# Rebuilding the state-space parameters in wider instructions, and moving the last modulation steps of a four-layer block program behind the next norm

## The chip, the cores and the metric

The program runs on one core of a Trainium2 chip. The metric is the device time of one execution in microseconds (us). Five engines have an instruction queue each and run it in order: PE (matrix products; its weight loads are shown as PEld), DVE (vector), ACT (scalar functions and copies), POOL and SP. In this program SP issues the weight loads (DMA queue q1) and POOL issues small and modulation loads (q0). Engines wait for each other by semaphores; an instruction that waits holds back everything behind it on its engine.

## The reference, cut to what matters

One sequence of 256 tokens with 1024 features goes through two *first* layers and then through a *second* block of two layers.

```python
# first block, two layers
h = rms_norm(x, pre_norm[l]);  proj = h @ w_in[l]          # attention and long convolution on parts of proj
x = x + rms_norm(m @ w_out[l], post_norm[l])               # the end of a first layer
# second block
def adaln(c, w, b):                                        # "modulation": 3072 columns, four times
    m = silu(c) @ w + b;  return split(m, 3)               # shift, scale, gate
x = x + g * even_mixer(rmsnorm(x) * (1 + sc) + sh, ...)    # layer 0: attention mixer
x = x + g * swiglu(rmsnorm(x) * (1 + sc) + sh, ...)        # layer 0: dense FFN, width 2816
x = x + g * s5_mixer(rmsnorm(x) * (1 + sc) + sh, ...)      # layer 1: state-space mixer
x = x + g * moe_swiglu(rmsnorm(x) * (1 + sc) + sh, ...)    # layer 1: 8 experts
```

The state-space mixer scans `x_t = a x_{t-1} + (f b) u_t` with complex `a`, `f`, `b`, reads out with complex `c` and adds `d_skip * u`. The kernel works on four tokens at a time and needs, from `a, f, b, c, d`, four tables per quarter q of the groups: B (input weights times powers of a), C (output weights times powers of a), K (the direct effect of the tokens of one group of four on each other, a product of C and B plus the diagonal d) and T (rotations). They depend on parameters only, not on x.

## The kernel before, in words

Stages follow each other in time: first layer 0 (to about 288 us), first layer 1 (to 562), even mixer (to about 725), dense FFN (to about 946), state-space mixer (to about 1056), experts (to the end). The 256 tokens are two tiles `tt` of 128. A projection (`proj_tok`, `proj_T`) loads weights by `wchunk` (raw tile by DMA from SP, high part `whi` on ACT at L208, rest `wlo` on DVE at L211) and runs each product as three matmuls, L221 to L223, from `hTh`, `hTl` (high part and rest of the transposed input) and `whi`, `wlo`.

**Between two stages** stands a norm. `x_done(tt)` computes row statistics of tile tt, makes the diagonal `dg` (L421) and lets PE transpose and scale x by it (`transposed`, L440: 8 instructions per tile, 16 records, since each such product is run in two passes). The result goes through `hh` into `hTh` (ACT) and `hTl` (DVE), and the next stage's matmuls can start. `hold` and `held` make the splits of the next stage's first weight chunks issue only after a given ACT instruction: before, the last row statistics of tile 1, for two chunks (`HOLDP` is 2 for a plain norm, `HOLDC` 0 for the one before the state-space mixer).

**Side tasks** are generators. `tick()` in the projections' loops advances each by its rate, `finish()` runs them to their end. One is `modulations()`: for each of the four modulations it runs `adaln`. There, eight times, three weight tiles `rawm` of 128x1024 are loaded by POOL (L945; only three such buffers exist), 24 matmuls with 32-column weights multiply them into four column groups of PE (L959, 48 records), ACT copies the sums to `ads` (L963), and POOL sends them by four small DMAs to `adp` (L965). After the eighth, PE transposes `adp` (L970), DVE forms the columns (L971 to L975) and PE transposes them once more (L977). Another side task is `s5_params`, which runs in the dense FFN and builds the four tables, one quarter after another; its K product is L1500: per quarter 16 matmuls with 128x128 weights and 32 moving columns, 32 records.

**The order** on each engine is set when the kernel is built: a scheduler with a timeline of its own places the instructions, in the order of emission where nothing else decides; `issue_after` and `gate` tie instructions to others, and `first()` gives priority.

## Time and profile before

| | us |
|---|---|
| median of three runs | 1911.8 (1909.59 to 1914.67) |
| the profiled execution | 1902.7 |
| its span, first to last instruction | 1900.2 |
| PE busy in the span | 1818.4 (96%) |
| DVE busy | 1554.9 (82%) |
| ACT busy | 1213.4 (64%) |
| POOL busy | 164.6 (9%) |
| mean granted PE clock, share of full | 0.965 |

The profiled execution is 9.1 us shorter than the median of the runs. A row of the timeline has start and length of a piece of work, engine, line, operation, the tiles `out<-in`, shapes, how many records are put together (x), and, in brackets, how long the engine had been idle before it and what ended that. Matmul records overlap: the pace of PE is read from the starts. A matmul with 512 moving columns starts every 0.23 us at full clock, one with 256 every 0.117 us.

### The profile page before, as it was taken

Reading aid. Unit: us, or ns where it says so; the run is one execution under the profiler, and the core shown is the slowest. Engines: PE = TensorE matmul, PEld = TensorE weight load, DVE = VectorE, ACT = ScalarE, POOL = GpSimd, SP = SyncE. Lnnn points to the kernel's source line nnn. Section 1 sums busy time; section 2 is a strip of 40 time slices with the busy share of each in tenths; the row PEclk is TensorE's granted clock in tenths of the full one; section 3 lists DMA queues with packets and bytes.
Section 4 is the critical chain, followed back from the end, with each engine's and each line's share of the span. In section 5 each row is a group of like instructions: output and inputs, shape, how many; then the busy total and the mean of one; then the engine's idle time right before and its main releaser. Section 6 shows DMA issues by size and latency. Waiting matters only on the chain.

```text
span 1900.2 us, 31269 instructions
## 1 busy us (share of the span) xinstructions
PE 1818.4 (96%) x11358; PEld 1551.7 (82%) x11358; DVE 1554.9 (82%) x2646; ACT 1213.4 (64%) x1708; POOL 164.6 (9%) x297
## 2 busy tenths in 40 slices
PE   7999998999989998999989899999999999999996
PEld 6887776988878778999889788888888888888784
DVE  6887667687558669998678789999999999998996
ACT  5664355564448535555554677887778787877774
POOL 0003232231330000000000100000001000100000
PEclk9999998999999969999988999999999999999998
DMA  7656785876775504787675779999999999999990
GB/s 247 205 153 209 245 286 197 277 259 196 255 242 159 165 22 156 227 270 241 208 284 196 279 266 376 340 355 344 378 342 349 353 377 354 346 369 361 339 352 24
DMA packets 258539, 503.58 MB, mean 265 GB/s; under 512 B 23346, under 2 KB 101108, under 8 KB 256328
## 3 DMA queue, kind: packets, MB, share of 16 engines
q1 hardware_dynamic: 239384, 448.05, 68.7%
q0 software_dynamic: 18992, 53.45, 7.9%
q8 instruction: 91, 1.49, 0.3%
q14 instruction: 72, 0.59, 0.1%
HBM read 485.47 MB, written 15.75 MB: 264 GB/s over the span
## 4 chain that ended last, share of the span: by engine, by line
PE 78%; issue 10%; DVE 6%; DMA 4%; ACT 2%; POOL 0%; POOLq 0%; ACTq 0%; DVEq 0%
PE A L222 12%; PE A L221 12%; PE A L223 12%; PE B L221 6%; PE B L222 6%; PE B L223 6%; PE A L323 4%; PE A L325 4%; PE A L324 4%; PE B L959 2%; DMA rawm<-in_e_mod_mix_w_dram 2%; DVE wlo L211 1%; PE B L1754 1%; PE B L1101 1%; PE B L440 1%
## 5 line engine op out<-in xcount | busy, mean ns | idle before, releaser
L211 DVE TENSOR_TENSOR wlo<-raw,whi 128x1024 fp32r<-128x1024 f32 x777 | 930.8, 1222 | 183.7 <-ACT whi L208 172.0
L208 ACT ACTIVATE whi<-raw 128x1024 fp32r<-128x1024 f32 x777 | 814.3, 1058 | 344.6 <-PE A L223 137.7
L221 PE MATMUL A<-whi,hTh 128*128 128x512 f32 (+1 forms) x752 | 286.7, 389 | 7.5 <-ACT hTh L208 4.9
L222 PE MATMUL A<-wlo,hTh 128*128 128x512 f32 (+1 forms) x752 | 290.0, 386 | 1.3 <-DVE wlo L211 1.0
L223 PE MATMUL A<-whi,hTl 128*128 128x512 f32 (+1 forms) x752 | 287.5, 384 | 0.9 <-DVE hTl L211 0.9
L323 PE MATMUL A<-hTh,whi 128*128 128x256 f32 x864 | 246.2, 285 | 3.5 <-ACT hTh L208 2.6
L325 PE MATMUL A<-hTh,wlo 128*128 128x256 f32 x864 | 245.2, 284 | 0.0
L324 PE MATMUL A<-hTl,whi 128*128 128x256 f32 x864 | 244.1, 283 | 1.0 <-DVE hTl L211 1.0
L221 PEld LDWEIGHTS A<-whi,hTh 128*128 128x128 f32 x752 | 142.9, 190 | 38.8 <-ACT hTh L208 6.1
L323 PEld LDWEIGHTS A<-hTh,whi 128*128 128x128 f32 x864 | 165.4, 192 | 6.9 <-ACT hTh L208 2.8
L222 PEld LDWEIGHTS A<-wlo,hTh 128*128 128x128 f32 x752 | 143.1, 190 | 33.9 <-DVE wlo L211 4.8
L223 PEld LDWEIGHTS A<-whi,hTl 128*128 128x128 f32 x752 | 142.6, 190 | 31.2 <-DVE hTl L211 2.1
L324 PEld LDWEIGHTS A<-hTl,whi 128*128 128x128 f32 x864 | 165.3, 191 | 3.2 <-DVE hTl L211 1.2
L325 PEld LDWEIGHTS A<-hTh,wlo 128*128 128x128 f32 x864 | 165.1, 191 | 1.7 <-issue 1.2
L222 PE MATMUL A<-wlo,xg 128*128 128x512 f32 (+1 forms) x384 | 143.1, 373 | 0.3 <-DVE wlo L211 0.3
L223 PE MATMUL A<-whi,xg 128*128 128x512 f32 (+1 forms) x384 | 142.7, 372 | 0.0
L221 PE MATMUL A<-whi,xg 128*128 128x512 f32 (+1 forms) x384 | 141.2, 375 | 0.0
L222 PE MATMUL B<-wlo,mhh 128*128 128x512 f32 x352 | 138.6, 394 | 0.0
L223 PE MATMUL B<-whi,mhl 128*128 128x512 f32 x352 | 137.5, 391 | 0.0
L221 PE MATMUL B<-whi,mhh 128*128 128x512 f32 x352 | 120.6, 393 | 0.2 <-ACT mhh L208 0.2
L222 PEld LDWEIGHTS A<-wlo,xg 128*128 128x128 f32 x384 | 72.3, 188 | 13.4 <-DVE wlo L211 0.8
L223 PEld LDWEIGHTS A<-whi,xg 128*128 128x128 f32 x384 | 72.3, 188 | 12.5
(588 smaller groups left out, 2868.9 us busy)
## 6 DMA issues: line engine op xcount, KB each, us to landing
raw<-in_o_exp_up_dram SPq DMA_DIRECT2D x176, 512.0 KB, 5.7
raw<-in_o_exp_down_dram SPq DMA_DIRECT2D x176, 512.0 KB, 6.0
raw<-in_o_exp_gate_dram SPq DMA_DIRECT2D x174, 512.0 KB, 5.8
raw<-in_w_in_dram SPq DMA_DIRECT2D x96, 512.0 KB, 4.8
rawm<-in_e_mod_mix_w_dram POOLq DMA_DIRECT2D x24, 512.0 KB, 6.0
rawm<-in_e_mod_ffn_w_dram POOLq DMA_DIRECT2D x24, 512.0 KB, 5.7
rawm<-in_o_mod_mix_w_dram POOLq DMA_DIRECT2D x24, 512.0 KB, 5.6
rawm<-in_o_mod_ffn_w_dram POOLq DMA_DIRECT2D x24, 512.0 KB, 6.3
```

The lines of the kernel that those rows point to most:

```text
L208: nc.scalar.activation(hi, src, AF.Copy)
L211: (nc.gpsimd if lo_eng == "pool" else nc.vector).tensor_tensor(lo, src, hi.bitcast(F32), ALU.subtract)
L221: nc.tensor.matmul(out, ah, bh, start=first, stop=False)
L222: nc.tensor.matmul(out, ah, bl, start=False, stop=False)
L223: nc.tensor.matmul(out, al, bh, start=False, stop=last)
L323: nc.tensor.matmul(o, wh[:, ms], xh[:, k, :], start=k == 0 and m == 0, stop=False, **kw)
L324: nc.tensor.matmul(o, wh[:, ms], xl[:, k, :], start=False, stop=False, **kw)
L325: nc.tensor.matmul(o, wl[:, ms], xh[:, k, :], start=False, stop=k == 7, **kw)
L440: nc.tensor.matmul(o, x[:, ks], dg, start=True, stop=True)
L959: nc.tensor.matmul(acc[32 * j:32 * j + 32, cs], silu[:, k:k + 1].broadcast_to([P, 32]), raws[i][:, k * P:(k + 1) * P], start=r == 0 and i ...
L1101: nc.tensor.matmul(pt[:, i, :], z[ps, ts], w[ps, ts], start=True, stop=True)
L1754: nc.tensor.transpose(ptr[:, i * P:(i + 1) * P], sg[:, i * P:(i + 1) * P], self.ident)
```

## The change

1. `s5_params`: the complex products that were made power by power are made for three or four powers in one instruction (128x384, 128x512), T for two quarters at once (`TQ` = 2); masks are applied by ACT while it copies; the tables' transposes are copied out of PSUM by ACT, not DVE. K is now 16 matmuls per quarter with 32-column weights and 128 moving columns, in four column groups of PE; it is written by 16 small DMAs per quarter from POOL, not by one from SP.
2. The projection `w_out` at the end of both first layers runs `quiet`: no `tick()` in it. After layer 0 one modulation step follows; at layer 1 the `finish(self.adalns)` ahead of the projection is gone, and all steps left are emitted behind the norm that follows, without priority (`urgent` false).
3. `hold` is now the last ACT instruction of tile 0's `transposed`; the first chunk's split is spared from it, the next two are held.

```diff
+    def finish_step(self, gen):
+        for t in list(self.tasks):
+            if t[0] is gen:
+                self.step(t)
@@ wchunk
-            with self.tc.issue_after(self.hold) if self.held > 0 else nullcontext():
+            with self.tc.issue_after(self.hold) if self.held > 0 and self.spared <= 0 else nullcontext():
                 self.split(hi, lo, raw, lo_eng="pool" if self.pool_lo >= 0 else "dve")
-            self.held -= 1
+            if self.spared > 0:
+                self.spared -= 1
+            else:
+                self.held -= 1
@@ proj_tok
-                if k0 + kk < kt and not (trail and c + wd == ncols):
+                if k0 + kk < kt and not (trail and c + wd == ncols or quiet):
                     self.tick()
-            self.tick()
+            if not quiet:
+                self.tick()
@@ x_done
             if tt:
-                self.hold, self.held = self.latest(mybir.EngineType.Activation), HOLDP if kind == "plain" else HOLDC
+                self.hold, self.held, self.spared = self.behind0, HOLDP if kind == "plain" else HOLDC, 1
             self.transposed(tt, x, dg)
+            self.behind0 = self.latest(mybir.EngineType.Activation)
@@ first_layer
-        if l == 1:
-            self.finish(self.adalns)
-        self.proj_tok(mT, a["w_out"][l], 0, D, 8, emit_out, trail=True)
+        self.proj_tok(mT, a["w_out"][l], 0, D, 8, emit_out, trail=True, quiet=True)
+        if l == 0:
+            self.urgent = False
+            self.finish_step(self.adalns)
+            self.urgent = True
@@ first_block
+            self.urgent = False
+            self.finish()
             self.gate = []
-            self.finish()
@@ adaln
-            with self.first():
+            with self.first(self.urgent):
@@ s5_params, B and the products
-            for s in range(3):
-                p = pw[:, 3 - s]
-                self.cmul(sp, [P, 8, 16], bc(p[:, 0, :], 16), bc(p[:, 1, :], 16), W[:, 0, :, 3, :], W[:, 1, :, 3, :],
-                          W[:, 0, :, s, :], W[:, 1, :, s, :], "s5cm")
+            self.cmul(sp, shape, *p, *w, W[:, 0, :, 0:3, :], W[:, 1, :, 0:3, :], "s5cw")
-                V.tensor_tensor(B[:, i:i + 2].rearrange("p a b c -> p (a b) c"), pt.rearrange("p (n c) -> p n c", n=4),
-                                bm[:, None, 0, :].broadcast_to([P, 4, P]), ALU.mult)
+                nc.scalar.copy(B[:, i:i + 2].rearrange("p a b c -> p (a b) c"), pt.rearrange("p (n c) -> p n c", n=4))
@@ s5_params, K
-            for i in range(8):
+            for h in range(2):
                 for ri in range(2):
-                    nc.tensor.matmul(pt[:, i * 32:(i + 1) * 32], W2[:, ri, i].rearrange("p s g k -> p (s g k)"),
-                                     cm[:, ri, i].rearrange("p g k -> p (g k)"), start=ri == 0, stop=ri == 1)
+                    for i in range(4):
+                        nc.tensor.matmul(pt[32 * i:32 * i + 32, h * P:(h + 1) * P], W2[:, ri, 4 * h + i, 3].rearrange("p g k -> p (g k)"),
+                                         C[:, 4 * h + i, ri, 0:4].rearrange("p t g k -> p (t g k)"), start=ri == 0, stop=ri == 1,
+                                         skip_group_check=True)
-            self.dq.dma_start(self.sK[q], K.rearrange("p a b -> p (a b)"))
+                for i in range(4):
+                    self.mq.dma_start(self.sK[q][s * 32:(s + 1) * 32].rearrange("k (h i m) -> k i h m", h=2, i=4)[:, i],
+                                      K[i * 32:(i + 1) * 32, :, 3 - s:7 - s].rearrange("k h t m -> k h (t m)"))
```

In the changed kernel some lines have other numbers: L959 is L973, L440 is L450, L221 to L223 are L226 to L228, L970 and L977 are L984 and L991, L945 is L959, L963 and L965 are L977 and L979.

**PE between first layer 1 and the even mixer, before.** From the last `w_out` matmul on: `adp` and `adb` are the modulation's two transposes, `dg,x` the norm's transposes of tile 0, `whi_6487` and so on the chunks of the mixer's first weights.

```order
L223 MATMUL A_6273<-whi_6306,hTl_6083 128x512
L970 MATMUL B_6180<-ident_78,adp_5451 128x96
L977 MATMUL B_6187<-ident_78,adb_5448 8x128
L440 MATMUL B_6385<-dg_6383,x_75 128x128 x4
L440 MATMUL B_6397<-dg_6383,x_75 128x128 x4
L221 MATMUL A_6483<-whi_6487,hTh_6365 128x512
L222 MATMUL A_6483<-wlo_6488,hTh_6365 128x512
L223 MATMUL A_6483<-whi_6487,hTl_6366 128x512
```

**The same place on PE in the changed kernel**, from the second tile's transposes on; ahead of them stand tile 0's transposes and six matmuls of `whi_6487`. `rawm` are the modulation weights.

```order
L450 MATMUL B_6341<-dg_6327,x_75 128x128 x4
L973 MATMUL B_6353<-rawm_6041,silu_1264 32x128 x8
L973 MATMUL B_6353<-rawm_6040,silu_1264 32x128 x8
L973 MATMUL B_6353<-rawm_6039,silu_1264 32x128 x8
...
L973 MATMUL B_6390<-rawm_6386,silu_1264 32x128 x8
L973 MATMUL B_6390<-rawm_6385,silu_1264 32x128 x8
L973 MATMUL B_6390<-rawm_6384,silu_1264 32x128 x8
L973 MATMUL B_6427<-rawm_6423,silu_1264 32x128 x8
L973 MATMUL B_6427<-rawm_6422,silu_1264 32x128 x8
L973 MATMUL B_6427<-rawm_6421,silu_1264 32x128 x8
L984 MATMUL B_6458<-ident_78,adp_5584 128x96
L226 MATMUL A_6483<-whi_6493,hTh_6248 128x512
```

Three modulation groups and the transpose of `adp`, which stood ahead of the last `w_out` matmul or right behind it, now stand in front of all of the mixer's matmuls but twelve (six ahead of these rows, six where "..." stands).

**POOL at that place in the changed kernel** (its DMA issues; `mgt` is a gate row).

```order
L206 DMA mgt_6480<-rowe_mod_mix_1259 128x1024
L959 DMA rawm_6384<-in_o_mod_ffn_w_dram 128x1024
L959 DMA rawm_6385<-in_o_mod_ffn_w_dram 128x1024
L959 DMA rawm_6386<-in_o_mod_ffn_w_dram 128x1024
L979 DMA adp_5584<-ads_6378 3x1x128 x4
L959 DMA rawm_6421<-in_o_mod_ffn_w_dram 128x1024
L959 DMA rawm_6422<-in_o_mod_ffn_w_dram 128x1024
L959 DMA rawm_6423<-in_o_mod_ffn_w_dram 128x1024
L979 DMA adp_5584<-ads_6415 3x1x128 x4
L979 DMA adp_5584<-ads_6452 3x1x128 x4
```

Each `rawm` issue waits until PE has read the tile that it overwrites: the second group's loads wait for the first group's matmuls, the third's for the second's.

**PE between the even mixer and the dense FFN.** Before, both tiles' transposes stood in a row, and no matmul of the FFN between them:

```order
L440 MATMUL B_7925<-dg_7923,x_75 128x128 x4
L440 MATMUL B_7937<-dg_7923,x_75 128x128 x4
L440 MATMUL B_7997<-dg_7995,x_75 128x128 x4
L440 MATMUL B_8009<-dg_7995,x_75 128x128 x4
```

In the changed kernel 25 matmuls of tile 0 (12 of `whi_8037`, 12 of `whi_8043`, one of `whi_8049`) stand between them; its ends are:

```order
L450 MATMUL B_7941<-dg_7927,x_75 128x128 x4
L226 MATMUL A_8059<-whi_8037,hTh_7909 128x256
L227 MATMUL A_8059<-wlo_8038,hTh_7909 128x256
...
L228 MATMUL A_8059<-whi_8043,hTl_7910 128x256
L226 MATMUL A_8059<-whi_8049,hTh_7909 128x256
L450 MATMUL B_8001<-dg_7999,x_75 128x128 x4
```

The first weight chunks are split earlier, and tile 0's matmuls no longer wait for tile 1.

## Rows read from the trace of the kernel before

**Rows 1.** Busy time of each engine in first layer 1 and the dense FFN, by stretch.
```profile
core 0: us, PE busy (x) PEld busy (x) DVE busy (x) ACT busy (x) POOL busy (x), PEclk, DMA share, GB/s
300.00:550.00 250.00, 249.97 (x2238) 213.11 (x2238) 171.59 (x316) 129.40 (x214) 70.45 (x137) 0.99 0.75 250
750.00:900.00 150.00, 150.00 (x1094) 141.45 (x1093) 138.41 (x403) 88.25 (x141) 3.65 (x12) 0.99 0.76 248
```

**Rows 2.** Timeline of PE around one K product in the dense FFN.
```profile
785.99 3.89 PE L1500 MATMUL B<-s5cmk,s5W 128*128 128x32 f32 x32
789.70 0.56 PE L323 MATMUL A<-hTh,whi 128*128 128x256 f32 x1
```

**Rows 3.** Timeline of PE around one modulation group in first layer 1.
```profile
543.61 0.40 PE L222 MATMUL A<-wlo,hTh 128*128 128x512 f32 x1
543.84 0.40 PE L223 MATMUL A<-whi,hTl 128*128 128x512 f32 x1
544.17 1.52 PE L959 MATMUL B<-rawm,silu 128*32 128x128 f32 x48
545.62 0.50 PE L221 MATMUL A<-whi,hTh 128*128 128x512 f32 x1
```

**Rows 4.** Timeline of PE from first layer 1 into the even mixer.
```profile
555.66 1.52 PE L959 MATMUL B<-rawm,silu 128*32 128x128 f32 x48 [1.13 <-DMA rawm<-in_o_mod_ffn_w_dram]
...
562.34 0.40 PE L223 MATMUL A<-whi,hTl 128*128 128x512 f32 x1
563.71 0.27 PE L970 MATMUL B<-ident,adp 96*128 96x96 f32 x1 [0.96 <-PE A L223]
564.84 0.27 PE L977 MATMUL B<-ident,adb 128*8 128x128 f32 x1 [0.87 <-DVE sm L333]
566.56 3.00 PE L440 MATMUL B<-dg,x 128*128 128x128 f32 x16 [1.45 <-DVE sm L342]
572.13 0.79 PE L221 MATMUL A<-whi,hTh 128*128 128x512 f32 x1 [2.57 <-ACT whi L208]
...
574.13 0.63 PE L223 MATMUL A<-whi,hTl 128*128 128x512 f32 x1
574.55 0.63 PE L221 MATMUL A<-whi,hTh 128*128 128x512 f32 x1
...
579.99 0.48 PE L222 MATMUL A<-wlo,hTh 128*128 128x512 f32 x1
```

**Rows 5.** Timeline of PE in first layer 0: two modulation groups that waited.
```profile
198.16 1.52 PE L959 MATMUL B<-rawm,silu 128*32 128x128 f32 x48 [0.79 <-DMA rawm<-in_e_mod_mix_w_dram]
...
206.09 1.52 PE L959 MATMUL B<-rawm,silu 128*32 128x128 f32 x48 [0.53 <-DMA rawm<-in_e_mod_mix_w_dram]
```

**Rows 6.** Timeline of POOL: the loads issued between those two groups.
```profile
199.12 1.62 POOL L945 DMA_DIRECT2D rawm<-in_e_mod_mix_w_dram  x3 [7.26 <-PE B L959]
```

**Rows 7.** Timeline of ACT: the copy behind the last modulation group.
```profile
557.23 0.49 ACT L963 ACTIVATE ads<-B 128x384 f32<-128x384 f32 x1 [3.25 <-PE B L959]
```

**Rows 8.** Timeline of DVE: a weight split at the start of the even mixer.
```profile
572.26 1.22 DVE L211 TENSOR_TENSOR wlo<-raw,whi 128x1024 fp32r<-128x1024 f32 x1
```

**Rows 9.** Timeline of PE from first layer 0 into layer 1.
```profile
298.98 0.79 PE L221 MATMUL A<-whi,hTh 128*128 128x512 f32 x1 [2.65 <-ACT hTh L208]
```

**Rows 10.** Timeline of ACT at the same place.
```profile
295.47 2.94 ACT L208 ACTIVATE whi<-raw 128x1024 fp32r<-128x1024 f32 x3
```

**Rows 11.** Timeline of DVE at the same place, a filter step ahead of tile 0's statistics.
```profile
286.64 0.74 DVE L594 SCALAR_TENSOR_TENSOR k<-k,col,k 128x512 f32<-128x512 f32 x1
```

**Rows 12.** Timeline of PE from the even mixer into the dense FFN.
```profile
732.70 3.78 PE L440 MATMUL B<-dg,x 128*128 128x128 f32 x16 [5.04 <-DVE dg L421]
736.13 0.56 PE L221 MATMUL A<-whi,hTh 128*128 128x256 f32 x1
...
738.14 0.28 PE L221 MATMUL A<-whi,hTh 128*128 128x256 f32 x1
```

**Rows 13.** Timeline of ACT at the same place.
```profile
728.80 3.90 ACT L208 ACTIVATE whi<-raw 128x1024 fp32r<-128x1024 f32 x4
```

More of the change, by code (lines that the diff above doesn't have):

```diff
@@ L1489, in s5_params @@
[L1489 to L1496 removed]
+            C = self.t(sp, [P, 8, 2, 5, 2, 16], "s5C")
@@ new lines, in s5_params @@
+            shape = [P, 8, 4, 16]
+            p = [pw[:, 1:5, ri, qs].rearrange("p t i -> p i t")[:, :, :, None].broadcast_to(shape) for ri in range(2)]
+            c = [craw[:, ri, :, None, :].broadcast_to(shape) for ri in range(2)]
+            cr, ci = self.t(sp, shape, "s5cr"), self.t(sp, shape, "s5ci")
+            self.cmul(sp, shape, *p, *c, cr, ci, "s5cw", neg_i=True)
+            for ri, v in enumerate((cr, ci)):
+                for g in range(2):
+                    copy(C[:, :, ri, 0, g, :], craw[:, ri], 2 * ri + g)
+                    copy(C[:, :, ri, 1:5, g, :], v, g)
@@ new lines, in s5_params @@
+            yield
+            if q % TQ == 0:
+                n8 = 8 * TQ
+                T = self.t(sp, [P, 3, n8, 64], "s5T", bufs=1)
+                nc.gpsimd.memset(T[:, 0, :, 0:1], 1.0)
+                nc.gpsimd.memset(T[:, 1, :, 0:1], 0.0)
+                ts = slice(q * 8, q * 8 + n8)
+                bt = lambda v, n: v[:, ts, None].broadcast_to([P, n8, n])
+                for k in range(6):
+                    n = 1 << k
+                    self.cmul(sp, [P, n8, n], T[:, 0, :, :n], T[:, 1, :, :n], bt(ca[:, k + 1, :], n), bt(sa[:, k + 1, :], n),
+                              T[:, 0, :, n:2 * n], T[:, 1, :, n:2 * n], "s5cw")
+                    if k == 4:
+                        yield
+                nc.scalar.copy(T[:, 2], bt(mg4, 64))
+                nc.gpsimd.memset(T[:, 2, :, 0:1], 0.0)
+                for k in range(TQ):
+                    self.dq.dma_start(self.sT[q + k].rearrange("p (a i c) -> p a i c", a=3, i=8), T[:, :, 8 * k:8 * k + 8])
+                yield
```

93 lines of the change are left out of this document (32 added, 61 removed).

## The prediction

> **What bounds the kernel now.** I read the busy times by stretch first. In the two stages in which most of the moved work lies, first layer 1 and the dense FFN, PE is busy for the whole stretch: 249.97 of 250 us and 150.00 of 150 us, at 0.99 of the full clock [rows 1]. DVE comes next (138.41 of 150 in the FFN), but no wait of PE for it stands there: the matmuls start one behind the other. So a microsecond of PE work taken out of the FFN is a microsecond gained, and DVE, ACT or POOL work taken out is worth nothing by itself. Then I read PE's timeline where one stage ends and the next begins, since only there PE stands still: from first layer 0 to 1, from first layer 1 to the even mixer, from there to the FFN [rows 4, 9, 12]. The experts, 44% of the time, are not touched.
>
> **Part 1, the state-space tables.** The K product takes PE from 785.99 to 789.70, 3.71 us for 32 records, 0.116 us each [rows 2]; there are four such groups, 14.8 us. The changed form is that of the modulation groups: 32-column weights, 128 moving columns, four column groups. One of those starts at 544.17 and the stream goes on at 545.62: 1.45 us for 48 records, 0.030 us each [rows 3]. Thirty-two take 0.97 us, four groups 3.9 us. Around such a group the first start is 0.33 us behind the last, where the stream's own distance is 0.23 [rows 3]; 0.1 us on either side of four groups is 0.8. Part 1 gives 14.8 - 3.9 - 0.8 = 10.1 us; I take **-9.5**, since the K group before may hold a little of the normal spacing (0.23 x 4 = 0.9 at most, half of it). Bounds: 0, if the four column groups do not run beside each other and a record costs 0.116 as before, and -10.9, without the cost of entry. The shorter DVE work is the cover for this gain: PE at the faster pace asks for its splits earlier, and DVE at 92% would be the next to bind, but its products fall to fewer instructions. The 64 small K writes lie on POOL, busy 3.65 of 150 us [rows 1], and are read only in the next stage: nothing.
>
> The Trainium skill (TensorEngine Tiling (Array Packing), Key Properties) says that changing the tiling mode drains the array, which speaks against putting 32-column products into a stream of 128-column ones. The trace shows that price as the 0.1 us above; if it were a whole record's 0.40 us on either side instead, part 1 would give 7.7 us.
>
> **Part 2, the end of layer 0.** PE waits 2.65 us for `hTh` [rows 9], because ACT made three weight splits, 2.94 us, ahead of it [rows 10]. In the new order two of them stand behind `hTh`, and the spared one falls where ACT was idle: the 2.94 us go. DVE runs two filter steps of some 0.74 us ahead of tile 0's statistics [rows 11]; with a quiet projection they are elsewhere, 1.5 us. Against that the spared chunk's `wlo`, 1.22 us [rows 8], now stands inside tile 0's chain. Together **-3.2**, from -5 to -1. The work that leaves the projection goes into layer 1, where POOL, ACT and DVE have room.
>
> **Part 3, from the even mixer to the FFN.** ACT makes four splits, 3.90 us, ahead of `hTh` [rows 13], and PE waits 5.04 us for tile 1 without a matmul of the FFN [rows 12]. Now 25 matmuls of tile 0 stand in between: 25 x 0.117 (half of a 512-column one's 0.23, [rows 3]) = 2.9 us that PE does in its wait. The nine matmuls from 736.13 to 738.14 ran at half clock, 0.22 us each [rows 12]; with no such wait ahead that is 0.9 less. **-3.7**, from -5 to -1.
>
> **Part 4, from layer 1 to the even mixer.** This decides the sign. Call 562.34, the last `w_out` matmul, zero. Before, the mixer's first matmul starts at +9.8, and at +17.65 (579.99) PE is at full pace with 13 done [rows 4]. Now, step by step:
> - Tile 0's transposes start as before, at +4.2. Its matmuls come a split (1.1 us) earlier, at +8.7. Six of them at half clock (0.42, [rows 4]) end at +11.3. Tile 1's transposes take 2 us: +13.4.
> - Then PE meets the first of three modulation groups; its weights are there. The second's loads wait for it, the third's for the second. Between two groups that waited for their loads lie 206.09 - 198.16 = 7.93 us [rows 5]: 0.96 to the issue, 1.62 of issuing [rows 6], the rest transfer. The second starts at +21.3, the third at +29.3. Six matmuls of tile 1 fit into the first of these waits.
> - From the last group to the transpose of `adp` it was 563.71 - 555.66 = 8.05 us [rows 4], with the copy to `ads` in it [rows 7], and PE did wait for it at the end. So +37.3. All behind it on PE waits, and ACT has put the next split behind all three copies to `ads`.
> - The columns on DVE (about 1 us, as between the two transposes in [rows 4]) and `wlo`, 1.22 us [rows 8]: full supply at +39.5, with 14 matmuls done.
>
> That is 39.5 - 17.65 = 21.9 us later, less 0.2 for the one matmul more, and 1.6 more since some eight matmuls behind so long a wait run at half clock (0.42 and not 0.23, [rows 3, 4]): 23.3. In return three groups of 1.45 us and the wait of 1.13 us [rows 4] leave the time ahead of zero: -5.5. Sum **+18**. Low end +12: 7 us from group to group, which is an estimate from the same rows for a queue with nothing else on it, the tiles 1 us earlier, no half clock. High end +23: 9.5 us from group to group, between 7.93 and the 11.5 us of the last two groups (544.17 to 555.66, [rows 3, 4]), under other loads.
>
> The Trainium skill (DMA: Bandwidth & Descriptors, Anatomy of one DMA) gives 2.0 us and bytes over 436 GB/s for one such DMA; worked out for the three, 1.57 MB, that is an estimate of 5.6 us from issue to landing. The rows show 206.09 - 199.12 = 7.0 us to the next matmul. By the page part 4 would be some +15.
>
> **Sum.** -9.5 - 3.2 - 3.7 + 18 = +1.6 us. The scheduler also places the first 250 us of work in another order; the work is the same, and I take 0, within 3 either way. From the profiled execution's 1902.7 us that gives 1904.3. It lies 9.1 us under the median of the runs, 1911.8, so the median should be **1913.4**.
>
> **Rivals.**
> - *The fetches are short.* With nothing else on the queue the two loads and the round trip of `adp` cost less: +12 in part 4, the rest as summed: -4.4, 1907.4; with the joins at their better ends (-5, -5) -7.5, 1904.3. For it: SP has little to load while PE stands still. Against it: 2.6 us of each 7.93 pass before the last transfer is even issued. With the other ways to a gain, such as a DVE relief in the FFN that the timeline doesn't show, 0.30.
> - *The fetches are long*, slower than before: the third load and `adp` see the 9.5 us above, +23 in part 4, so +6.6: 1918.4. It decides for the slower side from about 9 us between groups. For it: the last two groups needed 11.5. Against: weights were loading then. 0.16.
> - *The column groups don't run beside each other* in the FFN (a K record still 0.116 us): part 1 gives nothing, +11: 1922.9. Against it stand the 0.030 us of rows 3 for the same shape. 0.10.
> - *The change does nothing here*: PE waits at none of these places, part 4 falls away with its credit. Excluded as far as the order goes: PE takes its queue in order, and the two loads can't be issued before the groups ahead of them.
>
> **How the numbers follow.** A difference under 0.3%, 5.7 us, can't be told from none. The forecast, with the sum between -5.7 and +5.7, has 0.42; the fast rival falls mostly beyond -5.7 with the joins' better ends, 0.30; the two slow rivals and what else is late in the reordered stages, 0.28. The likeliest alone gives 1907 to 1918; for 8 in 10 the range takes in the short fetches with the best joins and a bit of the early reordering, 1901, and the failed column groups, 1923.
>
> **What would show it.** PE idle before the second and third modulation group of the join, about 6 and 7 us, ended by `rawm` DMAs, and before the transpose of `adp`, about 6 us; the four K groups about 1 us each; 25 FFN matmuls between the two tiles' transposes. It would be wrong if PE met those groups with the weights already there, if the K groups took 3 us, or if a new wait stood in the FFN, ended by ACT's copies of `s5W` or `s5C`.

## The result

| | before | changed |
|---|---|---|
| median of the runs, us | 1911.9 (1909.59 to 1914.67) | 1927.5 (1925.51 to 1928.59) |
| ratio to before | | 1.008 [1.0062, 1.0097] |
| profiled execution, span, us | 1900.2 | 1926.7 |
| PE busy / DVE busy in the span, us | 1818.4 / 1554.9 | 1821.7 / 1521.4 |

The changed kernel is 0.8% slower; the forecast was 1913.4, with 1901 to 1923 as its range. To see where the time went, take the start of the last matmul of each stage ahead of the norm that ends it, in PE's timeline (562.34 in [rows 4], 577.38 below; the modulations' own two transposes are not counted). The differences are the lengths of the stages. The execution profiled before was a quick one of its kernel, so the same kernel was run once more ("again", an execution of 1908.6 us, which is also the median of its runs):

| us | layer 0 | layer 1 | mixer | FFN | rest | span |
|---|---|---|---|---|---|---|
| before | 287.5 | 274.8 | 163.1 | 221.2 | 953.6 | 1900.2 |
| before, again | 289.2 | 273.9 | 168.9 | 219.9 | 954.4 | 1906.2 |
| changed | 288.8 | 288.6 | 197.2 | 204.3 | 947.9 | 1926.7 |
| changed less again | -0.4 | +14.7 | +28.3 | -15.6 | -6.5 | +20.5 |
| forecast | 0 | -8.7 | +23.3 | -13.2 | 0 | +1.6 |

(The forecast's credit of 5.5 us and part 2 lie in layer 1, its 23.3 in the mixer, parts 1 and 3 in the FFN; it took 23.3 - 5.5 as 18. One profiled execution stands for each kernel; that two of one kernel differ by 6 us in the mixer says how far one stage of one execution can be trusted.) The FFN and the mixer came out as the sum had them, a little larger each. **Layer 1 did not: 23 us off.**

**The join from layer 1 to the mixer, after.** PE's timeline, the counterpart of [rows 4] (start, length, engine, line, operation, tiles, shapes, records, and the idle time ahead with what ended it):

```profile
577.38 0.40 PE L228 MATMUL A<-whi,hTl 128*128 128x512 f32 x1
582.34 3.32 PE L450 MATMUL B<-dg,x 128*128 128x128 f32 x16 [4.57 <-DVE sm L351]
587.15 0.50 PE L226 MATMUL A<-whi,hTh 128*128 128x512 f32 x1 [1.49 <-ACT hTh L213]
...
589.60 2.02 PE L450 MATMUL B<-dg,x 128*128 128x128 f32 x16 [0.54 <-DVE dg L430]
591.55 1.52 PE L973 MATMUL B<-rawm,silu 128*32 128x128 f32 x48
...
600.57 2.79 PE L973 MATMUL B<-rawm,silu 128*32 128x128 f32 x48 [5.66 <-DMA rawm<-in_o_mod_ffn_w_dram]
609.67 2.79 PE L973 MATMUL B<-rawm,silu 128*32 128x128 f32 x48 [6.31 <-DMA rawm<-in_o_mod_ffn_w_dram]
617.18 0.40 PE L984 MATMUL B<-ident,adp 96*128 96x96 f32 x1 [4.72 <-DMA adp<-ads]
...
619.55 0.80 PE L227 MATMUL A<-wlo,hTh 128*128 128x512 f32 x1 [0.85 <-DVE wlo L216]
```

The three waits of the forecast stand there: 5.66 and 6.31 us for the loads of the second and third group, 4.72 for `adp`. From group to group it takes 9.02 and 9.10 us (forecast 7.93, high end 9.5), and the last wait is shorter (7.51 from group to transpose, forecast 8.05). Full supply is at 619.55 - 577.38 = 42.2, forecast 39.5. Unforeseen is that the second and the third group themselves run at half clock: 2.79 us, where 1.52 was usual, with a granted clock of 0.59 in 600 to 625:

```profile
core 0: us, PE busy (x) PEld busy (x) DVE busy (x) ACT busy (x) POOL busy (x), PEclk, DMA share, GB/s
600.00:625.00 25.00, 12.54 (x116) 9.39 (x117) 5.90 (x20) 5.35 (x8) 11.77 (x19) 0.59 0.38 108
```

**The K product, after,** in PE's timeline, the counterpart of [rows 2]:

```profile
828.78 0.40 PE L228 MATMUL B<-whi,fhl 128*128 128x512 f32 x1
829.12 1.08 PE L1519 MATMUL B<-s5C,s5W 128*32 128x128 f32 x32
830.13 0.39 PE L332 MATMUL A<-hTh,whi 128*128 128x256 f32 x1
```

It takes 1.01 us from start to start, 3.71 before, and the entry costs 0.34 - 0.23 = 0.11. That was the forecast.

**Layer 1.** PE's waits (line, what for, us in total, times, longest), first before (again, 290 to 564), then after (289 to 578):

```profile
PE B L440 <- DVE sm L342: 4.7, 1, 4.7
PE A L221 <- ACT hTh L208: 2.8, 1, 2.8
PE B L959 <- DMA rawm<-in_o_mod_ffn_w_dram: 1.0, 1, 1.0
```
```profile
PE B L450 <- DVE dg L430: 4.2, 1, 4.2
PE A L332 <- ACT whi L213: 3.8, 1, 3.8
PE B L973 <- DMA rawm<-in_o_mod_mix_w_dram: 3.6, 2, 3.0
PE A L334 <- DVE wlo L216: 1.7, 2, 1.2
PE A L226 <- DVE k L887: 1.1, 1, 1.1
PE A L227 <- DVE wlo L216: 0.8, 1, 0.8
PE B L973 <- DMA rawm<-in_e_mod_ffn_w_dram: 0.7, 1, 0.7
PE B L589 <- ACT k L213: 0.6, 1, 0.6
```

Before, PE waits only at the join at its start (4.7 and 2.8) and once for a modulation's loads. After, part 2 did its work: the 2.8 for `hTh` is gone. But nine smaller waits, 12.3 us in all (one more of 0.2 is not shown), stand behind it, and the half clock behind them (granted clock 0.72 in 360 to 370 and 0.83 in 400 to 410, where the run again of before shows 1.00 from 340 to 540). The waits together grew from 8.5 to 16.7 us. The other 6.5 of the 14.7 us are PE at work for longer, with about the same work (19 modulation groups in place of 20, one filter step more); how much of this is the clock was not taken apart. The largest wait can be followed through the queues; ACT, then SP and POOL, then PE:

```profile
364.09 0.63 ACT L585 ACTIVATE k<-k 128x512 f32<-128x512 f32 x1 [3.87 <-DMA k<-in_flt_deltas_dram]
364.62 1.04 ACT L213 ACTIVATE whi<-raw 128x1024 fp32r<-128x1024 f32 x1
```
```profile
353.98 1.63 POOL L959 DMA_DIRECT2D rawm<-in_e_mod_ffn_w_dram  x3 [9.53 <-PE B L973]
```
```profile
355.01 0.38 SPq L270 DMA_DIRECT2D raw<-in_w_in_dram  x1
355.44 0.50 SPq L584 DMA_DIRECT2D k<-in_flt_deltas_dram  x1
```
```profile
365.71 0.58 PE L332 MATMUL A<-hTh,whi 128*128 128x256 f32 x1 [3.76 <-ACT whi L213]
```

A filter step stands at the head of ACT's queue and waits for its decay rates. They were asked for at 355.44, behind 0.5 MB of weights and next to 1.5 MB of modulation weights from 353.98, and are there 8.6 us later. The weight split behind it on ACT starts right after it, with no wait of its own; PE waits for that split. Before has the same four steps for this layer, but their rates are asked for at 276, 303, 337 and 370 us (again), the first still in `w_out` of layer 0; here it is 324, 339, 355 and 397, all four in layer 1 and three of them within 31 us.

### The profile page after: what moved, and what is told of

The parts are those of the page before. It is cut to its first block, busy times and chain, and to the rows that moved or that the text cites. A ratio compares the mean times of both kernels' runs of the same rounds, so it can differ in the third digit from the quotient of the medians.

```text
span 1926.7 us, 31051 instructions
## 1 busy us (share of the span) xinstructions
PE 1821.7 (95%) x11358; PEld 1545.8 (80%) x11358; DVE 1521.4 (79%) x2393; ACT 1209.0 (63%) x1669; POOL 196.3 (10%) x355
## 4 chain that ended last, share of the span: by engine, by line
PE 75%; issue 10%; DVE 7%; DMA 5%; ACT 2%; POOL 1%; SPq 0%; ACTq 0%; DVEq 0%; POOLq 0%
PE A L227 12%; PE A L226 12%; PE A L228 12%; PE B L226 6%; PE B L227 6%; PE B L228 6%; PE A L334 3%; PE A L332 3%; PE A L333 3%; PE B L973 2%; DVE wlo L216 2%; PE B L1115 1%; DMA rawm<-in_o_mod_mix_w_dram 1%; PE B L1770 1%; ACT whi L213 1%
## 5 line engine op out<-in xcount | busy, mean ns | idle before, releaser
L226 PE MATMUL A<-whi,hTh 128*128 128x512 f32 (+1 forms) x752 | 284.3, 387 | 4.9 <-ACT hTh L213 4.9
L228 PE MATMUL A<-whi,hTl 128*128 128x512 f32 (+1 forms) x752 | 287.2, 384 | 0.7 <-DVE hTl L216 0.6
L226 PEld LDWEIGHTS A<-whi,hTh 128*128 128x128 f32 x752 | 142.2, 189 | 35.3 <-ACT hTh L213 6.3
L228 PEld LDWEIGHTS A<-whi,hTl 128*128 128x128 f32 x752 | 142.2, 189 | 31.3 <-DVE hTl L216 2.4
L228 PE MATMUL A<-whi,xg 128*128 128x512 f32 (+1 forms) x384 | 142.9, 372 | 0.0
L226 PE MATMUL A<-whi,xg 128*128 128x512 f32 (+1 forms) x384 | 141.6, 376 | 0.0
L228 PE MATMUL B<-whi,mhl 128*128 128x512 f32 x352 | 137.5, 391 | 0.0
L226 PE MATMUL B<-whi,mhh 128*128 128x512 f32 x352 | 120.8, 393 | 0.2 <-ACT mhh L213 0.2
L228 PEld LDWEIGHTS A<-whi,xg 128*128 128x128 f32 x384 | 72.4, 189 | 12.6
```

Of the source, the lines that this page charges most:

```text
L226: nc.tensor.matmul(out, ah, bh, start=first, stop=False)
L228: nc.tensor.matmul(out, al, bh, start=False, stop=last)
```

## The experiments

"Layers" is the sum of layers 0 and 1 (before again 563.1, changed 577.4). Each kernel's order is made anew, so an edit moves more than itself.

**Which part costs.** Before, unchanged, as a yardstick.

> The kernel before, profiled once more. The profiled execution on which the prediction was made lies 9 us under the median of the runs; its even mixer took 163 us from the last output-projection matmul of layer 1 to that of the mixer, where four other kernels with the same mixer work took 171 to 172. Theory (that execution was granted the full clock earlier in the mixer's attention part): this one takes about 171 there and 1908 to 1913 in all, other stages within 2 us. Rival (the changed state-space part makes the mixer ahead of it slower): 163 again, and the 9 us lie in another stage.

1908.6, ratio 0.9995 [0.9974, 1.0016]: no difference. The mixer is 168.9, nearer to the theory's 171 than to the rival's 163.

Before with only the state-space part, as a diff from the changed kernel:

```diff
-    self.hold, self.held, self.spared = self.behind0, HOLDP if kind == "plain" else HOLDC, 1
+    self.hold, self.held = self.latest(mybir.EngineType.Activation), HOLDP if kind == "plain" else HOLDC
...
+    if l == 1:
+        self.finish(self.adalns)
-    self.proj_tok(mT, a["w_out"][l], 0, D, 8, emit_out, trail=True, quiet=True)
+    self.proj_tok(mT, a["w_out"][l], 0, D, 8, emit_out, trail=True, quiet=False)
-    if l == 0:
-        self.urgent = False
-        self.finish_step(self.adalns)
-        self.urgent = True
...
-    self.urgent = False
-    self.finish()
     self.gate = []
+    self.finish()
```

> The kernel before with only the state-space part changed (larger products, K in column groups, small K writes). All theories say that the moved steps have nothing to do with this part. Theory (PE paces the dense FFN): the K groups fall from 3.7 to 1.0 us each, the stretch from the norm ahead of the FFN to the norm ahead of the state-space mixer falls by 9.5 to 13 us, the whole by as much: about 1900 where before is 1912. Rival (the FFN gain of the changed kernel, 17 us in its trace, is all of part 1, since shorter DVE work also counts): 15 to 17 us, about 1896. Rival (nothing of it survives, the next stages give it back): 1910 to 1912.

1891.5, 0.9902 [0.988, 0.9924]. FFN 208.7 against 219.9: -11.2 (forecast -9.5). The time fell by more than this stage and below all that was expected: layer 0 is 3.6 shorter as well and the rest 4.5, though no state-space work lies in layer 0. A new order and the program's end (see the last section) are in these; they were not taken apart.

The same with the new hold, that is, that diff without its first two lines:

```diff
     self.hold, self.held, self.spared = self.behind0, HOLDP if kind == "plain" else HOLDC, 1
```

> The changed kernel with both ends of the first layers as before: ticks in both output projections, modulations finished ahead of the second. The state-space part and the new hold stay. Theory (the loss is made of the moved side work alone: stalls in first layer 1 and the serial loads behind it): both losses go, the FFN gain and some 3 to 4 us at the norm ahead of the FFN and a little at the other norms stay, so 14 to 19 us under before: 1893 to 1898. Rival (the new hold is what hurts in first layer 1 and in the mixer): near before or slower, 1910 to 1920.

1894.3, 0.9919 [0.9898, 0.9939]. The hold shortens the FFN by 4.1 more, to 204.6 (forecast 3.7), but layer 0 is 292.8 against 285.6. In its waits stand two in layer 0 which the kernel without the hold does not have:

```profile
PE B L558 <- ACT k L548: 3.4, 1, 3.4
PE A L226 <- DVE k L887: 3.2, 1, 3.2
```

So the early part of the program, which the forecast took as "the work is the same", paid for the hold. In the changed kernel the same two waits stand, 3.4 and 3.2, and the quiet end hides them in the length of layer 0.

The changed kernel with layer 1's end as before:

```diff
+    if l == 1:
+        self.finish(self.adalns)
-    self.proj_tok(mT, a["w_out"][l], 0, D, 8, emit_out, trail=True, quiet=True)
+    self.proj_tok(mT, a["w_out"][l], 0, D, 8, emit_out, trail=True, quiet=l == 0)
...
```

> The changed kernel, but first layer 1 ends as before (ticks in its projection, modulations finished ahead of it); layer 0 keeps its quiet projection. Theory: the three groups with their loads leave the join to the mixer, where PE stood some 26 us longer at the price of 5.5 earlier: about 20 us under the changed kernel, 1906 to 1910. The stalls of PE in first layer 1 (about 12 us of waits from 340 to 400, filter steps on ACT and one load) stay. Rival (those stalls come from the modulations left to the end, not from layer 0's quiet projection): they go too, 1890 to 1896.

1909.5, 0.9993 [0.9972, 1.0014]: 18 us less than the changed kernel. (The profiled execution took 1901.9, 7.6 less than the median of its runs, so its stages add up to a larger gain.) The mixer is 171.0 (197.2), but layer 1 is still 285.1 with layer 0 at 288.3. One group of the 285.1 stands behind the last `w_out` matmul (283.1 up to there), with its weights nearly there: PE waits 0.4 us for it. So layer 1 is long without any group that waits at the join.

Then with layer 0's end as before:

```diff
-    self.proj_tok(mT, a["w_out"][l], 0, D, 8, emit_out, trail=True, quiet=True)
+    self.proj_tok(mT, a["w_out"][l], 0, D, 8, emit_out, trail=True, quiet=l == 1)
-    if l == 0:
-        self.urgent = False
-        self.finish_step(self.adalns)
-        self.urgent = True
```

> The changed kernel, but layer 0 ends as before (ticks in its projection, no single step behind it); layer 1 keeps its quiet projection and the modulations behind the norm. Theory (filter steps pushed out of layer 0 starve layer 1: ACT stands at a filter step whose load is late, weight splits behind it): PE's waits of 3.8, 1.2 and 3.0 us around 350 to 400 go and first layer 1 is 12 to 18 us shorter, the join from 0 to 1 some 4 us longer, and only two groups are left behind layer 1: 1905 to 1916. Rival (the stalls come from something else): first layer 1 stays as long as in the changed kernel, 1920 to 1930.

1906.7, 0.9978 [0.9964, 0.9992]: 20.7 less. Layer 1 is 269.4, shorter than before and about as forecast, layer 0 295.0; the layers 564.4. Only two groups are left for the join, which makes the mixer 185.9. **The quiet end of layer 0 is what lengthens layer 1.** The other kernels bear it out: with the task's rate unchanged, layer 1 takes 269.4 to 275.9 in all seven profiled executions where layer 0 ends as before, and 278.9 to 294.0 in the five where it ends quiet and layer 1 keeps its loads.

**Whose ticks are missing in layer 0?** The filter's alone given back to its `w_out`, then the modulations' alone (there without the step behind the norm); `quiet` names the tasks that may go on:

```diff
...
-    self.proj_tok(mT, a["w_out"][l], 0, D, 8, emit_out, trail=True, quiet=True)
+    self.proj_tok(mT, a["w_out"][l], 0, D, 8, emit_out, trail=True, quiet=(lambda: self.filters) if l == 0 else True)
```
```diff
...
-    self.proj_tok(mT, a["w_out"][l], 0, D, 8, emit_out, trail=True, quiet=True)
+    self.proj_tok(mT, a["w_out"][l], 0, D, 8, emit_out, trail=True, quiet=(lambda: [self.adalns]) if l == 0 else True)
```

> The changed kernel, but in layer 0's output projection the filter task still ticks; the modulations do not. Theory (filter steps pushed into first layer 1, with their loads behind weight loads on SP and weight splits behind them on ACT, starve PE): the waits of 3.8, 1.2 and 0.5 us around 350 to 367 and the half clock behind them go, first layer 1 falls from 288.6 to about 276 to 280 us, the whole to 1914 to 1919. Rival (the modulations kept back starve it): first layer 1 stays at 285 to 290, the whole at 1924 to 1930.

1923.1, 1.0066 [1.0046, 1.0086]; layer 0 293.6, layer 1 277.3, the layers 570.9.

> The changed kernel, but in layer 0's output projection the modulations still tick, at their old rate, without the single step behind it; the filter task does not. Theory (filter steps starve first layer 1): it stays near 285, and only the end behind layer 1 gets shorter if one group less is left there, by 8 to 9 us: 1915 to 1922. Rival (the modulations kept back do it): first layer 1 falls to about 275 and the whole to 1900 to 1908.

1915.0, 1.003 [1.0017, 1.0044]; 293.8 and 277.5, the layers 571.3, and two groups at the join (mixer 185.5). Either one frees layer 1 of 11 us and costs layer 0 five. Neither theory holds alone. That both tasks must meet in layer 1 would fit, but it is not shown, since another order with both of them there frees nearly as much (the join, below).

**Is it their loads?** The decay rates asked for a step ahead in layer 1, into a buffer of their own (`deltas` makes it and issues the load):

```diff
+    early = self.deltas(l, 0, 0) if l else None
...
-    de = self.k2([P, 512])
-    self.dq.dma_start(de, a["flt_deltas"][l, c0:c0 + 512].partition_broadcast(P))
+    de = early if l else self.deltas(l, o, dr)
...
+    if l and o + dr < 2:
+        early = self.deltas(l, o + dr, 1 - dr)
```

> The changed kernel, but the filter of layer 1 asks for its decay rates one step ahead, into a buffer of their own, so that ACT's absolute value of them finds them there. In the changed kernel ACT waits 3.87 us for that load at 364 us of the profiled execution, a weight split behind it on ACT, and PE waits 3.76 us for the split and runs at half clock behind. Theory (that load at the head of ACT's queue is a third of what layer 1 lost): layer 1 is 6 to 8 us shorter, the time 1918 to 1922. Rival (the queues of layer 1 are full: if this wait goes, another step of the side work is late at the same place): layer 1 within 3 us of the changed kernel's 288.6, the time 1924 to 1930.

1927.6, 1.0087 [1.0061, 1.0114]; layer 1 286.4. The edit missed its aim: two filter steps now stood close together, and with one buffer the second load could be asked for only at 346.42; ACT waited longer than in the changed kernel:

```profile
356.87 0.63 ACT L591 ACTIVATE kde<-kde 128x512 f32<-128x512 f32 x1 [8.70 <-DMA kde<-in_flt_deltas_dram]
```

It says nothing of the theory, so the loads were taken away instead. The rates loaded once and used in all four steps:

```diff
...
+    if l == 0 or o + dr == 0:
         self.dq.dma_start(de, a["flt_deltas"][l, c0:c0 + 512].partition_broadcast(P))
         nc.scalar.activation(de, de, AF.Abs)
```

> The changed kernel, but the filter of layer 1 loads its decay rates once and uses the same ones in all four steps (so that its filters are not the reference's): ACT has no load of them to wait for in layer 1. Theory (ACT's wait for that load, with weight splits queued behind it, is a part of its own of what layer 1 lost): layer 1 is 6 to 9 us shorter than the changed kernel's 288.6, the time 1918 to 1922. Rival (the side work is late somewhere else then): layer 1 within 3 us, the time 1924 to 1930.

Layer 1 280.0, 8.6 less, as the theory had it, and ACT has no such wait. The whole time is 1924.8 (1.008 [1.0053, 1.0107]), 2.7 less than the changed kernel: layer 0 is 1.7 longer, and the rest, with the same code, 3.9 longer in this execution (1.9 of it at the program's end, see the last section). The stage agrees, the total does not reach the expected 1918 to 1922.

The modulation groups in layer 1 without loads:

```diff
-    if m0 + bufs < 24:
+    if m0 + bufs < 24 and (key == "e_mod_mix" or key == "o_mod_ffn" and m0 + bufs >= 18):
         raws = fetch(m0 + bufs)
```

> The changed kernel, but the modulation groups that lie in layer 1 use weights that are already there (some 10 MB of loads fall away there; those modulations' values are not the reference's); the matmuls, copies and small DMAs of these groups stay, and so do the loads at the join to the even mixer. Theory (the DMA queues: layer 1 loses its time because modulation, filter and weight loads share them): layer 1 gets back to 274 to 279, the time 1912 to 1918. Rival (order and place of the side work in the queues of ACT and DVE): layer 1 at 284 or more, the time 1922 to 1928.

1914.5, 1.0032 [1.0013, 1.0051]: 13 less, with the 19 groups' matmuls, copies and small DMAs still there. Far more than the expected 10 MB fell away: POOL issues 39 loads of 0.5 MB in place of 96, so 30 MB less, and in layer 1 only 6 of 57 are left. Layer 1 is 276.1 (theory 274 to 279). All of PE's waits in it (283 to 559.5) are now:

```profile
PE B L450 <- DVE dg L430: 4.2, 1, 4.2
PE A L227 <- DVE wlo L216: 1.9, 3, 0.9
PE B L589 <- ACT k L213: 1.6, 1, 1.6
PE B L973 <- issue: 0.7, 1, 0.7
PE A L226 <- ACT hTh L213: 0.6, 2, 0.3
PE B L589 <- DVE fT L567: 0.3, 1, 0.3
```

9.3 us, about as many as before has (8.5). Layer 0 is also 5.6 shorter, which two groups' loads less there and the new order share in a way that this run does not tell. Without the loads, the modulations' or the filter's, most of layer 1's loss goes (12.5 and 8.6 of 14.7). **That the loads must go for this is not shown:** each edit also made a new order, and a run further on (the join) keeps all 57 loads in layer 1 and loses 9.7 of the 14.7 by its order alone, with 10.6 us of waits.

The new hold taken out of the first block (`late_hold` is set where the second block begins):

```diff
-    self.hold, self.held, self.spared = self.behind0, HOLDP if kind == "plain" else HOLDC, 1
+    if not self.late_hold:
+        self.hold, self.held = self.latest(mybir.EngineType.Activation), HOLDP if kind == "plain" else HOLDC
+    else:
+        self.hold, self.held, self.spared = self.behind0, HOLDP if kind == "plain" else HOLDC, 1
```

> The changed kernel with the new hold in the second block's norms only; the norm between the layers of the first block holds its first splits as before. Theory (the hold costs some 6 us in the first block here too, as it did without the quiet projections): layers 0 and 1 together 4 to 7 us shorter than the changed kernel's 577.4, the time 1920 to 1924. Rival (with a quiet projection the splits are no longer late, and the hold then gains what was forecast): the same as the changed kernel or up to 3 us longer, 1926 to 1931.

1927.5, 1.0096 [1.0063, 1.0128]: nothing. Layer 0 is 8.3 shorter (280.5), the two waits there are gone, and layer 1 is 5.4 longer (294.0). The rival was right, though for another reason than it gave: what layer 0 gains, layer 1 mostly gives back.

**The join.** The last two groups without loads of their own:

```diff
-    if m0 + bufs < 24:
+    if m0 + bufs < (18 if key == "o_mod_ffn" else 24):
```

> The changed kernel, but the second and third modulation group of the last modulation use the weights that are already there, so that no load stands between the three groups at the join from layer 1 to the even mixer (that modulation's values are not the reference's). Theory (the two waits of about 6 us for the loads are what the join costs): the two waits go, what is left is the round trip of the adp rows, full supply comes some 13 to 17 us earlier, and the time is 1910 to 1914. Rival (the round trip, the place in PE's queue and the half clock behind cost as much without the loads): 1921 to 1928.

1914.3, 1.0035 [1.0017, 1.0053]. The total is at the theory's edge, but for two reasons. The three groups run in one (4.14 us), and PE then waits for the round trip of `adp`:

```profile
583.96 4.14 PE L973 MATMUL B<-rawm,silu 128*32 128x128 f32 x144
598.04 0.39 PE L984 MATMUL B<-ident,adp 96*128 96x96 f32 x1 [8.35 <-DMA adp<-ads]
```

POOL shows why that wait grew from 4.72 to 8.35: the copies to `ads` share one buffer, and POOL issues their rows one group after another, 3.9 us apart.

```profile
586.76 1.98 POOL L979 DMA_DIRECT2D adp<-ads  x4 [12.59 <-ACT ads L977]
590.71 1.97 POOL L979 DMA_DIRECT2D adp<-ads  x4 [1.96 <-ACT ads L977]
594.58 1.98 POOL L979 DMA_DIRECT2D adp<-ads  x4 [1.91 <-ACT ads L977]
```

So without the loads the mixer is only 10.0 shorter; another 9.7 of layer 1 went with the new order there (278.9), which was no part of the theory: layer 1 has the same groups, filter steps and 57 modulation loads in both kernels. The counterpart of the chain above shows what the order did (SP, POOL, ACT):

```profile
354.14 0.50 SPq L584 DMA_DIRECT2D k<-in_flt_deltas_dram  x1
```
```profile
355.81 1.63 POOL L959 DMA_DIRECT2D rawm<-in_e_mod_ffn_w_dram  x3 [8.48 <-PE B L973]
```
```profile
359.72 0.63 ACT L585 ACTIVATE k<-k 128x512 f32<-128x512 f32 x1 [0.63 <-DMA k<-in_flt_deltas_dram]
```

The rates are asked for behind the same 0.5 MB of weights, but 1.7 us ahead of the modulation's 1.5 MB and not 1.5 us behind them. They are there after 5.6 us in place of 8.6, ACT waits 0.63 us and not 3.87, and PE does not wait for the split. The same side work in another order can cost layer 1 ten microseconds less: its loss is not a fixed price of its amount, and which loads meet is a part of it.

**K alone.** Before with the state-space part, but K in its old form:

```diff
-    for h in range(2):
+    for i in range(8):
         for ri in range(2):
-            for i in range(4):
-                nc.tensor.matmul(pt[32 * i:32 * i + 32, h * P:(h + 1) * P], W2[:, ri, 4 * h + i, 3].rearrange("p g k -> p (g k)"),
...
+            nc.tensor.matmul(pt[:, i * 32:(i + 1) * 32], W2[:, ri, i].rearrange("p s g k -> p (s g k)"),
+                             C[:, i, ri, 0].rearrange("p g k -> p (g k)"), start=ri == 0, stop=ri == 1)
```

> The kernel before with only the new state-space part, but with the K product as it was (per quarter 16 matmuls with 128x128 weights and 32 moving columns; the K table it makes is not the reference's). All else of the new part stays: wider DVE instructions, masks and copies on ACT. Theory (the gain of the FFN is PE's, from the column groups): the four K groups take some 3.7 us again, the FFN is about 10.5 us longer than with the new K product alone, and the time is 1899 to 1905. Rival (the gain comes from DVE, which has fewer instructions): the time stays at 1889 to 1895.

1906.0, 0.9988 [0.9972, 1.0003], 1 us beyond the theory's time; FFN 219.9, to the tenth that of before. The K groups by line, here, and in the kernel with the whole state-space part (busy us, mean ns of one):

```profile
L1514 PE MATMUL B<-s5C,s5W 128*128 128x32 f32 x128 | 14.6, 273 | 0.0
```
```profile
L1515 PE MATMUL B<-s5C,s5W 128*32 128x128 f32 x128 | 4.3, 276 | 0.0
```

One matmul takes as long either way; in four column groups four run at a time. All of the FFN's gain is that. DVE is busy for 112.02 of 150 us in 750 to 900 here (138.41 in [rows 1]), and it gains nothing: the rival is out.

**The version that beats both.** The state-space part, and the new hold in the second block alone, on top of the kernel before with the state-space part:

```diff
+    if self.late_hold:
+        self.hold, self.held, self.spared = self.behind0, HOLDP if kind == "plain" else HOLDC, 1
+    else:
         self.hold, self.held = self.latest(mybir.EngineType.Activation), HOLDP if kind == "plain" else HOLDC
```

> The kernel with the new state-space part alone, and the new hold only at the norms of the second block, so at the one ahead of the dense FFN. Theory (the new hold costs some 6 us in first layer 0 and gains 4 ahead of the FFN): 3 to 5 us under the kernel with the state-space part alone, 1886 to 1889, and no other stage changed. Rival (the 4 us are given back in the FFN by its weight loads): 1891 to 1893.

1885.4, 0.9879 [0.9852, 0.9906]: layers 563.0, mixer 168.3, FFN 204.2. It keeps the two gains and none of the costs.

**What a modulation group costs in another place,** in that version, by the task's rate. At 80, 12 groups lie in layer 0 and 20 in layer 1; at 100 they are 16 and 16, at 70 (the second run) 9 and 23:

```diff
-ADALN_RATE = 80
+ADALN_RATE = 100
```

> The fastest version so far (the kernel before, the new state-space part, the new hold in the second block's norms alone: 1885.4), with the modulation task's rate raised so that all its 32 groups and the last adp round trip are done before the projection at the end of layer 1. Theory (what stands at the join is worth its place, earlier is free as long as few groups wait): the wait of PE for adp at that join and one group go, 1881 to 1884. Rival (16 groups in layer 0 wait for their rawm loads there): 1886 to 1892.

1922.9, 1.0068 [1.0046, 1.0091], 37 more than at 80. Layer 0 is 315.4 (287.1), and PE waits there for the modulations' loads, at 80 for 3.4 us:

```profile
PE B L972 <- DMA rawm<-in_e_mod_ffn_w_dram: 13.4, 2, 8.6
...
PE B L972 <- DMA rawm<-in_e_mod_mix_w_dram: 7.4, 3, 3.7
```

> The fastest version so far (1885.4) with a lower rate of the modulation task: 9 groups in layer 0 and 23 in layer 1, in place of 12 and 20; nothing is left for the join. Theory (what a group costs is its place: layer 1 can't take more of them without waits, as in the changed kernel): layer 0 4 to 8 us shorter, layer 1 8 to 15 longer, the time 1888 to 1895. Rival (the higher rate's 28 us in layer 0 show that groups are dear there and cheap in layer 1): 1878 to 1884.

1926.4, 1.0104 [1.0064, 1.0144]. The edit did not do what was expected of it: of the 23 groups only 18 lie in layer 1's stream. Five are left behind the last `w_out` matmul, at 560.78, and run bare ahead of the norm's transposes (609.99), four of them after a full round trip and at half clock:

```profile
560.78 0.40 PE L228 MATMUL A<-whi,hTl 128*128 128x512 f32 x1
562.61 1.52 PE L972 MATMUL B<-rawm,silu 128*32 128x128 f32 x48 [1.43 <-DMA rawm<-in_o_mod_ffn_w_dram]
571.44 2.79 PE L972 MATMUL B<-rawm,silu 128*32 128x128 f32 x48 [7.32 <-DMA rawm<-in_o_mod_ffn_w_dram]
581.19 2.79 PE L972 MATMUL B<-rawm,silu 128*32 128x128 f32 x48 [6.95 <-DMA rawm<-in_o_mod_ffn_w_dram]
589.78 2.79 PE L972 MATMUL B<-rawm,silu 128*32 128x128 f32 x48 [5.81 <-DMA rawm<-in_o_mod_ffn_w_dram]
598.53 2.79 PE L972 MATMUL B<-rawm,silu 128*32 128x128 f32 x48 [5.96 <-DMA rawm<-in_o_mod_ffn_w_dram]
```

Up to that `w_out` matmul layer 1 takes 270.2 (275.9 with 20 groups at 80); with the five groups it is 310.3. So the run does not say what more groups would cost in layer 1's stream, as its theory meant to ask; it prices the join a second time.

Both times came out far past the expected ones: there is no smooth price per group. A group with PE's own work around it costs its 1.45 us [rows 3]; one without cover costs 8.6 to 9.8 (here) or 9.0 to 9.1 (the join).

## Why the prediction was wrong, point by point

- **Part 1** (-9.5): right in kind; 11.2 measured, a little beyond the better bound of 10.9. No cover failed: DVE did not become the bound. The Trainium skill (TensorEngine Tiling (Array Packing), Key Properties) has the array drained at a change of tiling mode; the trace agrees only with a small price, 0.11 us at the entry. At a record's time on either side the gain would have been the 7.7 us of the prediction's working.
- **Part 3** (-3.7): right, 4.1 with the hold alone, by the mechanism named: PE works on tile 0 while tile 1 is made ready. Tile 1's transposes no longer wait.
- **Part 2** (-3.2): right at its place. PE goes from tile 0's transposes into six matmuls with no wait (`hTh` 2.65 before, [rows 9]).
- **Part 4** (+18): right, and slightly too small. Full supply came 2.7 us later than forecast, mostly because a group's round trip took 9.0 and 9.1 us instead of the 7.93 of [rows 5], the edge of the rival "the fetches are long". From a formula of the Trainium skill (DMA: Bandwidth & Descriptors, Anatomy of one DMA) the prediction worked out an estimate of 5.6 us for three such loads from issue to landing. The trace shows more: at the join it took 8.0 and 7.7 us from POOL's first issue (592.52 and 601.98) to the matmuls that waited. The two groups at half clock, 1.3 us more each, were not in the sum. With the mixer's half clock the stage is 28.3 longer, forecast 23.3; what part of these 5 us is the join's and what the execution's can't be told, since the mixer of unchanged code varied from 163.1 to 172.4.
- **The step that failed** is the last sentence of part 2: "The work that leaves the projection goes into layer 1, where POOL, ACT and DVE have room." Their busy shares in [rows 1] (POOL 70, ACT 129, DVE 172 of 250 us) do show room. But a queue that runs in order has room only if what is at its head can start; here ACT's head waited 3.87 us for a load, when POOL and SP had asked for 1.5 MB and 0.25 MB within 1.5 us, and PE waited 3.8 us behind it. That the work moved out of layer 0 lengthens layer 1 is shown (269.4 where layer 0 ends as before, 288.6 where it does not). How the loss divides among load waits, order and clock stays open. Layer 1 came out at +14.7 instead of -8.7, 23.4 us too long. The whole sum missed by 18.9 (+20.5 measured against the execution run again, +1.6 forecast): the mixer adds 5.0, and the FFN (-2.4), the rest (-6.5) and layer 0 (-0.4) take some of it back.
- **The zero for the early reordering** ("the work is the same, and I take 0, within 3 either way") failed as well, unseen in the total: the hold alone costs layer 0 some 7 us (292.8 against 285.6).
- **The rivals:** none of them had this mechanism. Fast fetches and the failed column groups are out (9.1 us a group; 1.01 us a K group). Long fetches came half true and would have given 1918.4.
- **The base:** the forecast carried 9.1 us from the profiled execution to the median. That was sound; most of it is the mixer, 163.1 in the profiled execution and 168.9 in the one at the median.

## What to carry to other kernels

Idle time of an engine is no room for work that begins with a load: ask what stands behind that load in the same queue and who waits for it, and count the loads that the moved work brings, not only its instructions, and which other loads are asked for just before them. Work that is made in small steps between matmuls must be priced by its cover: the same group costs 1.5 us inside a stream and some 9 us outside one. When every edit makes a new order, one edit is no proof of a cause: here a run that left a stage's work alone made that stage 9.7 us shorter. And a change of several parts is worth taking apart: here two parts gain 1.2% and the others lose more than that.

## What was not expected of the hardware

The same program spends a different time at half clock in the mixer from one execution to another. The granted clock in 655 to 680, 680 to 705 and 705 to 726 us was 0.86, 0.52 and 1.00 in the profiled execution of before and 0.73, 0.50 and 0.86 in the one run again (columns as in the window of the join; of each execution the first stretch):

```profile
655.00:680.00 25.00, 20.18 (x115) 15.40 (x114) 16.27 (x46) 7.10 (x18) 0.00 (x0) 0.86 0.14 43
```
```profile
655.00:680.00 25.00, 19.87 (x93) 14.84 (x95) 12.56 (x36) 6.47 (x18) 0.00 (x0) 0.73 0.14 47
```

Besides, the program's end takes a different time, with the same code. The last output's DMA is issued 9.6 us ahead of the end of the span in both executions of before (at 1890.59 of 1900.2 in the first) and 6.0 in the changed kernel (1920.75 of 1926.7). It is 5.9 to 6.0 in fourteen of the sixteen kernels with the new state-space part, but 7.9 and 10.4 in the other two (the rates loaded once, the modulation groups without loads), so the new part does not settle it. Why it is so stays open; 3.6 of the 6.5 us that the rest of the program gained lie there.
